# Attention products in two passes, returned pieces split a block earlier, and the sums of the weights sent by another queue

## The chip, the cores and the metric

The kernel runs on one core of a Trainium2 chip. The metric is device time in microseconds (us) for one execution, measured on the slowest core; here there is only one. Engines are called as in the profile: PE is the matrix engine (PEld its weight loads), DVE the vector engine, ACT the scalar engine, POOL the general-purpose engine, SP the engine that in this kernel issues the DMAs. Each has its own instruction queue and works it off in order.

## The reference

Two layers over a sequence of 1024 positions of width 1024, in float32. Layer 0 is a gated linear recurrence. Layer 1, where the change lies, is attention with 16 heads of 64 and a forget gate, and its own output gate:

```python
def fox_mixer(h, w_in, b_f, w_out):
    u = h @ w_in                                    # q, k, v, gate, forget logits
    cum = jnp.cumsum(jax.nn.log_sigmoid(f_logit), axis=1)
    # for each block of 128 queries:
    logits = jnp.einsum("bhqd,bhkd->bhqk", q_blk, kf) * scale
    logits = logits + (cq_blk[..., :, None] - ck[:, :, None, :])
    p = jax.nn.softmax(jnp.where(mask, logits, NEG_INF), axis=-1)
    o = jnp.einsum("bhqk,bkhd->bqhd", p, vf)
    ...
    return (o * jax.nn.silu(gate)) @ w_out
```

Both layers add their result to the residual, and a root-mean-square norm ends the program.

## The kernel before

Precision is kept by splitting: every operand of a large product is cut into a high part and a low part (`to_hi` on ACT, `to_lo` on DVE or POOL), and high times high, low times high and high times low are summed. For the product of attention weights with values, the high and low parts of one weight piece, `ph` and `pl`, are multiplied one after the other with the same stationary tile `v`, which holds high and low values side by side.

Layer 1 goes head by head (`hd` 0 to 15), each head in two halves of 512 queries (`c` = 0 and 1), each half in four rows of 128 queries. Two generators do the work of a half:

- `maxima(hd, c)` computes one row per step: logits `S` on PE, the masked row maximum on DVE (L775), the exponential with its row sum on ACT (L780). For the two longest rows of most halves, `turn_row` then transposes 32x32 blocks on DVE (L735), writes them to DRAM (`turnd`) and reads them back rearranged (`pp<-turnd`): these are the *returned* pieces, called far in the code. After the second half it inverts the eight row sums of the head, turns them on PE (`tr`, L793), copies them to `rc` (L795) and writes them to DRAM (`recd<-rc`, L796).
- `weigh(hd, c)` multiplies weights with values. Pieces of the two shorter rows (and the last piece of the others) are transposed on PE (`pt`), the other pieces come back by DMA. One step of it cuts one or two tiles of pieces into `ph` (ACT, L87) and `pl` (DVE, L98), and issues the products of the step before. `products` goes through the pieces of one step and issues, for each piece, its high product and then its low product into the accumulator `O`.

Between these runs `fill`: the projections of the next heads (`gps`), in steps of six 512-wide products. The order on PE is written out by hand: in a string, `0` is the next step of `weigh`, `1` the next row of `maxima`, `.` a step of fill and of a side task. `ORDER` holds two strings for heads 0 to 11: the first runs `weigh(hd, 0)` beside `maxima(hd, 1)`, the second `weigh(hd, 1)` beside `maxima(hd + 1, 0)`. `LAST` holds those of heads 12 to 15. `tc.issue_after` keeps the PE order as written; the order on ACT, DVE, POOL and SP is otherwise chosen when the program is built, by a planner that places an instruction when it expects its operands to be ready.

The sums come back later: `fetch_sums` (L805) reads `recd` into 64 partitions of `recb`, and `scale` (L815) multiplies the gate `sg` by it, on POOL, in two instructions; `gated` (L915), also on POOL, multiplies the head pair's result `yo` by `sg` after every second head. Both sums' transfers are issued by SP, which also issues every other transfer of the kernel. `settle` calls `fetch_sums` at its third step, behind a transfer of turned rows (`issue_after(written[0].ins)`), and `put_away` calls `scale` in the next head's first run.

Of the kernel before, what the change touches and what calls it, by code (L numbers as in the profile page):

```python
# [23 lines left out]
HD = 64  # L24
EPS = 1e-6
GROUP = 2
ORDER = "1.0..1.10.1.0", "10..1.0.10.10.0"
LAST = "1..0.1..10..1..0", "10..1.0..10..1.0..0"
NEG = -1e30
PSUM = bass.MemoryType.PSUM  # L30
# [8 lines left out]
def trunk(ctx: ExitStack, tc: tile.TileContext, xt, w0, wg, wo0, pc, gn, gf, w1, wv, wf, bf, wo1, out):  # L39
    nc = tc.nc  # L40
# [15 lines left out]
    def matmul(*args, **kw):  # L56
        pe[0] = nc.tensor.matmul(*args, **kw)  # L57
        return pe[0]
# [441 lines left out]
    recd = dram.tile([HEADS, 8, P], F32, name="recd")  # L500

    with ExitStack() as l1:
# [249 lines left out]
        def maxima(hd, c):  # L752

            s = hd % 2
            pair = hd // 2
            if c == 0:
                stats[hd] = at.tile([P, 16], F32, tag="sums", name="sums")[:, :8]
            sums = stats[hd]
            for i in reversed(range(4 * c, 4 * c + 4)):
                n = (i + 1) * P  # L760

                o_ = 192 if i == 4 else 0
                S = ps.tile([P, SEQ], F32, tag="S", name="S")[:, o_:]
                u = U[s][c]
                qs = slice(i % 4 * P, i % 4 * P + P)
                for lo_, hi_ in ((0, min(n, HALF - o_)), (HALF - o_, n)):
                    if hi_ <= lo_:
                        continue
                    hi_ = max(hi_, lo_ + 256)
                    matmul(S[:, lo_:hi_], u[:, 0, qs], T[s][:, 0, lo_:hi_], start=True, stop=False)  # L770
                    matmul(
                        S[:, lo_:hi_], u[:96, 1, qs], T[s][:96, 1, lo_:hi_], start=False, stop=True
                    )
                m = at.tile([P, 1], F32, tag="m", name="m", bufs=4)
                masked[0] = nc.vector.tensor_tensor_reduce(  # L775
                    S[:, :n], S[:, :n], mask[:, SEQ - n :], -1.0, -NEG, ALU.add, ALU.min, accum_out=m
                )

                p = ps_[i] = row_tile(i, n)
                seen[0] = nc.scalar.activation(  # L780
                    p, S[:, :n], AF.Exp, bias=m, scale=-1.0, accum_out=sums[:, i : i + 1]
                )
                if i % 4 > 1 and by_dma(hd, c):
                    turn_row(i, p)
                yield
            if hd == HEADS - 1 or c == 1:
                b0, b1 = (4 * c if hd == HEADS - 1 else 0), 4 * c + 4
                nb = b1 - b0
                sums = sums[:, b0:b1]
                nc.vector.tensor_scalar(sums, sums, 2.0, None, ALU.mult)  # L790
                nc.vector.reciprocal(sums, sums)
                tr = ps.tile([P, P], F32, tag="O", name="tr")
                nc.tensor.transpose(tr[:nb], sums, ident)  # L793
                rc = at.tile([8, P], F32, tag="rc", name="rc", bufs=1)
                nc.vector.tensor_copy(rc[:nb], tr[:nb])  # L795
                nc.sync.dma_start(recd[hd, b0:b1], rc[:nb])  # L796
                if hd > 13:
                    fetch_sums(hd, b0, b1)
                yield

        def fetch_sums(hd, b0=0, b1=8):
            pair, s = hd // 2, hd % 2
            if s == 0:
                recs[pair] = at.tile([P, SEQ], F32, tag="recb", name="recb", bufs=1)
            nc.sync.dma_start(  # L805
                recs[pair][s * HD : (s + 1) * HD, b0 * P : b1 * P],
                recd[hd : hd + 1, b0:b1].rearrange("o b q -> o (b q)").to_broadcast([HD, (b1 - b0) * P]),
            )
# [8 lines left out]
        def weigh(hd, c, sub=slice(0, HALF)):  # L817

            pair, s = hd // 2, hd % 2
            V = Vs[pair]  # L820
            if s == 0:
                yos[pair, c] = at.tile([P, HALF], F32, tag="yo", name="yo", bufs=2)
            yo = yos[pair, c][:, sub]
            O = ps.tile([P, HALF], F32, tag="O", name="O")[:, : sub.stop - sub.start]
            b = 4 * c

            def cover(r0, r1):
                first = [max(j, r0) for j in range(r1)]
                return [(j, (q - b) * P, (r1 - q) * P) for j, q in enumerate(first)]

            def packed(pieces):
                units = []
                for piece in pieces:
                    if not units or sum(w for _, _, w in units[-1]) + piece[2] > HALF:
                        units.append([])
                    units[-1].append(piece)
                return units

            if by_dma(hd, c):
                away = cover(b + 2, b + 4)  # L840
                mine = packed(cover(b, b + 2) + away[-1:])
                away = packed(away[:-1])
            else:
                mine, away = packed(cover(b + sub.start // P, b + sub.stop // P)), []
            steps = [(z[i : i + 2], z is away) for z in (mine, away) for i in range(0, len(z), 2)]
            count = [0, 2 * sum(map(len, mine + away))]

            later = []

            def products(units, parts, far):  # L850
                todo = []
                for unit, (ph, pl) in zip(units, parts):
                    at_ = 0
                    for j, q, w in unit:
                        cs = slice(at_, at_ + w)
                        (later if away and not far and j == b + 3 else todo).append((j, q, w, ph[:, cs], pl[:, cs]))
                        at_ += w
                if far:
                    todo[1:1] = later
                    later.clear()  # L860
                for j, q, w, *z in todo:
                    v = V[j][:, 2 * s : 2 * s + 2].rearrange("p a d -> p (a d)")
                    o = O[:, q - sub.start : q - sub.start + w]
                    for part in z:
                        matmul(o, v, part, start=count[0] == 0, stop=count[0] == count[1] - 1)
                        count[0] += 1

            held = None
            for units, far in steps:
                parts = [[at.tile([P, HALF], F32R, tag=t, name=t, bufs=3) for t in ("ph", "pl")] for _ in units]  # L870
                if not far:
                    A = ps.tile([P, 2, HALF], F32, tag="S", name="pt")
                srcs = []
                for u, unit in enumerate(units):
                    n = sum(w for _, _, w in unit)
                    parts[u] = [z[:, :n] for z in parts[u]]
                    if far:
                        k0, k1 = unit[0][0], unit[-1][0] + 1
                        srcs.append(far_rows(c)[:, :, k0:k1])
                        continue  # L880
                    srcs.append(A[:, u, :n])
                    i = 0
                    for j, q, w in unit:
                        for r in range(b + q // P, b + (q + w) // P):
                            transpose(A[:, u, i : i + P], ps_[r][:, j * P : (j + 1) * P], ident)
                            i += P

                def shaped(z):
                    return z.rearrange("p (k b q) -> p b k q", b=8, q=32) if far else z

                with tc.issue_after((seen if far else pe)[0].ins):
                    for (ph, pl), src in zip(parts, srcs):
                        to_hi(shaped(ph), src, nc.scalar)
                with tc.issue_after((masked if far else pe)[0].ins):
                    for (ph, pl), src in zip(parts, srcs):
                        to_lo(shaped(pl), src, shaped(ph), nc.vector)
                if held:
                    with tc.issue_after(pe[0].ins):
                        products(*held)
                held = units, parts, far  # L900
                yield
            products(*held)

            r0, r1 = s * HD, (1 - s) * HD
            nc.scalar.copy(yo[r0 : r0 + HD], O[r1 : r1 + HD])
            nc.vector.tensor_tensor(yo[r0 : r0 + HD], yo[r0 : r0 + HD], O[r0 : r0 + HD], ALU.add)
            yield
# [219 lines left out]
        for hd in range(HEADS):  # L1127
            pair = hd // 2
            if hd % 2 == 0:
                if hd < 12:  # L1130
                    fill = kq_units(pair + 1, ((1, (0, 1)), (0, (0,))))
                elif hd == 12:
                    pairs = ((0, 1), (2, 3), (4, 5), (6, 7))
                    todo = [(db, c) for two in pairs for c in range(2) for db in two]
# [127 lines left out]
```

## Time and profile before

| what | value |
|---|---|
| time, median of 3 runs | 1110.45 us (1110.2 to 1111.71) |
| the profiled execution, its own time | 1113.33 us |
| its span, first to last instruction | 1111.6 us |
| mean granted PE clock | 0.997 |
| busy: PE, DVE, ACT, POOL | 98%, 71%, 52%, 16% |
| the attention of heads 0 to 11 | about 512 to 941 us of the span |

The profile is one execution. A line of the timeline shows the start in us from the span's start, the length, engine, source line, operation, what it writes and reads, the shape, how many instructions are merged, and in brackets the idle time of the engine just before and what ended it. PE products are pipelined, so their lengths overlap: the distance from one start to the next is what a product costs.

### The profile page before, as it was taken

How to read it: one execution, taken by the hardware profiler on the slowest of the kernel's cores; microseconds unless marked ns; L12 is line 12 of the kernel's file. 1: busy time of each engine (PE TensorE's matmuls, PEld its weight loads, DVE VectorE, ACT ScalarE, POOL GpSimd, SP SyncE). 2: the span in 40 equal slices, each digit the busy share in tenths (PEclk: the TensorE clock that was granted, in tenths of full speed). 3: DMA queues.
4: the chain of work that ended last, by engine and by line, in shares of the span. 5: the costliest groups of instructions: out<-in, count | busy, mean ns of one | idle time of the engine just before them, and what ended most of it. 6: DMA issues, size and time to landing. Idle time of an engine off the chain costs nothing.

```text
span 1111.6 us, 15903 instructions
## 1 busy us (share of the span) xinstructions
PE 1088.2 (98%) x5645; PEld 921.9 (83%) x5645; DVE 785.4 (71%) x1280; ACT 581.3 (52%) x1037; POOL 175.2 (16%) x120
## 2 busy tenths in 40 slices
PE   9999999999999999999999999999999999999997
PEld 7787888888888888988888888888888889888876
DVE  7888755876568687757788477875678765666645
ACT  8487345355453665545555355553555544444435
POOL 2322212111212201420010200202002020110110
PEclk9999999999999999999999999999999999999999
DMA  6111111111112113446767347675376763885445
GB/s 220 62 52 43 51 54 48 43 54 45 49 45 75 48 55 127 130 113 165 199 204 195 116 139 195 198 198 146 107 204 195 202 170 100 251 294 182 138 148 189
DMA packets 100919, 145.81 MB, mean 131 GB/s; under 512 B 25348, under 2 KB 53636, under 8 KB 100840
## 3 DMA queue, kind: packets, MB, share of 16 engines
q1 hardware_dynamic: 100840, 144.80, 44.2%
q8 instruction: 44, 0.72, 0.3%
q14 instruction: 35, 0.29, 0.1%
HBM read 83.48 MB, written 36.11 MB: 108 GB/s over the span
## 4 chain that ended last, share of the span: by engine, by line
PE 75%; DMA 8%; DVE 7%; issue 5%; ACT 3%; SPq 1%; POOL 1%; ACTq 0%; DVEq 0%; POOLq 0%
PE gps L57 24%; PE ops L57 16%; PE ups L57 10%; PE vps L57 8%; PE O L57 5%; PE S L57 4%; PE gate L57 3%; PE turn L57 2%; DMA pp<-turnd 2%; PE pt L61 2%; DMA wf<-in_w 2%; DVE pl L98 2%; DMA turnd<-turn 1%; DVE turn L735 1%; DVE S L775 1%
## 5 line engine op out<-in xcount | busy, mean ns | idle before, releaser
L57 PE MATMUL gps<-hh,wh 128*128 128x512 f32 x576 | 229.8, 399 | 0.3 <-ACT wh L87 0.3
L57 PE MATMUL gps<-hh,wl 128*128 128x512 f32 x576 | 226.2, 393 | 0.0
L57 PE MATMUL gps<-hl,wh 128*128 128x512 f32 x576 | 225.3, 391 | 0.0
L87 ACT CAST wh<-wf 128x512 fp32r<-128x512 f32 (+2 forms) x156 | 94.5, 610 | 152.6 <-PE gps L57 47.8
L98 POOL TENSOR_TENSOR wl<-wf,wh 128x512 fp32r<-128x512 f32 (+1 forms) x60 | 101.9, 1705 | 376.0 <-ACT wh L87 261.4
L57 PEld LDWEIGHTS gps<-hl,wh 128*128 128x128 f32 x576 | 108.5, 188 | 23.5
L57 PEld LDWEIGHTS gps<-hh,wl 128*128 128x128 f32 x576 | 108.8, 189 | 19.6 <-POOL wl L98 0.2
L57 PEld LDWEIGHTS gps<-hh,wh 128*128 128x128 f32 x576 | 108.7, 189 | 19.4 <-ACT wh L87 0.6
L815 POOL TENSOR_TENSOR sg<-sg,recb 64x512 f32<-64x512 f32 x32 | 44.1, 1397 | 494.9 <-DMA recb<-recd 494.9
L775 DVE CUSTOM_DVE_ANT_0 S<-S,mask 128x512 f32<-128x512 f32 (+7 forms) x128 | 97.1, 758 | 25.4 <-PE S L57 24.9
L780 ACT ACTIVATE pp<-S,m 128x512 f32<-128x512 f32 (+1 forms) x64 | 54.4, 850 | 76.8 <-DVE m L775 76.3
L57 PE MATMUL S<-T,U 128*128 128x512 f32 (+7 forms) x384 | 91.4, 346 | 0.0
L57 PE MATMUL O<-pl,v 128*128 128x256 f32 (+3 forms) x302 | 80.3, 301 | 10.8 <-DVE pl L98 10.5
L98 DVE TENSOR_TENSOR wl<-wf,wh 128x512 fp32r<-128x512 f32 x96 | 64.9, 677 | 30.7 <-ACT wh L87 30.5
L375 DVE TENSOR_TENSOR x<-x,ops 128x512 f32<-128x512 f32 x80 | 54.1, 680 | 40.7 <-PE ops L57 40.7
L57 PE MATMUL O<-ph,v 128*128 128x256 f32 (+3 forms) x302 | 80.1, 289 | 1.3 <-ACT ph L87 1.3
L57 PEld LDWEIGHTS S<-T,U 128*128 128x128 f32 (+1 forms) x384 | 68.2, 189 | 12.6 <-ACT pp L780 0.6
L57 PE MATMUL ups<-hh,wl 128*128 128x512 f32 x192 | 75.3, 392 | 0.8 <-POOL wl L98 0.8
L57 PE MATMUL ups<-hh,wh 128*128 128x512 f32 x192 | 75.5, 394 | 0.4 <-ACT hh L89 0.4
L57 PE MATMUL ops<-yh,wh 128*128 128x512 f32 x192 | 75.2, 392 | 0.0
L57 PE MATMUL ups<-hl,wh 128*128 128x512 f32 x192 | 75.1, 391 | 0.1
L57 PE MATMUL ops<-yh,wl 128*128 128x512 f32 x192 | 74.7, 389 | 0.0
(170 smaller groups left out, 2361.8 us busy)
## 6 DMA issues: line engine op xcount, KB each, us to landing
wf<-in_w SPq DMA_DIRECT2D x100, 256.0 KB
turnd<-turn SPq DMA_DIRECT2D x26, 448.0 KB
pp<-turnd SPq DMA_DIRECT2D x52, 224.0 KB
wf<-in_wo SPq DMA_DIRECT2D x64, 128.0 KB
U<-qkh SPq DMA_DIRECT2D x64, 128.0 KB
T<-qkh SPq DMA_DIRECT2D x28, 256.0 KB
turnd<-turn SPq DMA_DIRECT2D x13, 384.0 KB
pp<-turnd SPq DMA_DIRECT2D x52, 96.0 KB
```

The lines of the kernel that those rows point to most:

```text
L57: pe[0] = nc.tensor.matmul(*args, **kw)
L61: pe[0] = nc.tensor.transpose(*args)
L87: nc.scalar.copy(hi, src)
L98: return eng.tensor_tensor(lo, src, f32(hi), ALU.subtract)
L375: nc.vector.tensor_tensor(x, x, pt, ALU.add)
L735: nc.vector.transpose(t[:, 0 if c else r].rearrange("p (m k q) -> p k m q", m=4, q=32), p[:, :n].rearrange("p (k m q) -> p k m q", m=4, q=32),
L775: masked[0] = nc.vector.tensor_tensor_reduce(S[:, :n], S[:, :n], mask[:, SEQ - n :], -1.0, -NEG, ALU.add, ALU.min, accum_out=m)
L780: seen[0] = nc.scalar.activation(p, S[:, :n], AF.Exp, bias=m, scale=-1.0, accum_out=sums[:, i : i + 1])
L815: nc.gpsimd.tensor_tensor(sg, sg, recs[hd // 2][rows, part], ALU.mult)
```

## The change

Three edits. In `products`, a step now issues the high products of all its pieces first and then the low products of all of them, instead of high and low of each piece in turn. In the first string of `ORDER`, the second step of `weigh(hd, 0)`, which cuts the returned pieces and issues the products of the pieces that PE transposed, stands after the second row of `maxima(hd, 1)` instead of after the third; the step of fill that stood between the second and the third row stands behind it. And both transfers of the sums (`recd<-rc` and `recb<-recd`) are issued by POOL's queue instead of SP's, for all 16 heads. An edge that `issue_after` sets binds instructions of the same engine, so the fetch is no longer placed behind the transfer of turned rows on SP.

```diff
-ORDER = "1.0..1.10.1.0", "10..1.0.10.10.0"
+ORDER = "1.0..10.1.1.0", "10..1.0.10.10.0"
...
                 rc = at.tile([8, P], F32, tag="rc", name="rc", bufs=1)
                 nc.vector.tensor_copy(rc[:nb], tr[:nb])
-                nc.sync.dma_start(recd[hd, b0:b1], rc[:nb])
+                nc.gpsimd.dma_start(recd[hd, b0:b1], rc[:nb])
...
-            nc.sync.dma_start(
+            nc.gpsimd.dma_start(
                 recs[pair][s * HD : (s + 1) * HD, b0 * P : b1 * P],
                 recd[hd : hd + 1, b0:b1].rearrange("o b q -> o (b q)").to_broadcast([HD, (b1 - b0) * P]),
             )
...
-                for j, q, w, *z in todo:
-                    v = V[j][:, 2 * s : 2 * s + 2].rearrange("p a d -> p (a d)")
-                    o = O[:, q - sub.start : q - sub.start + w]
-                    for part in z:
-                        matmul(o, v, part, start=count[0] == 0, stop=count[0] == count[1] - 1)
+                for part in range(2):
+                    for j, q, w, *z in todo:
+                        v = V[j][:, 2 * s : 2 * s + 2].rearrange("p a d -> p (a d)")
+                        o = O[:, q - sub.start : q - sub.start + w]
+                        matmul(o, v, z[part], start=count[0] == 0, stop=count[0] == count[1] - 1)
                         count[0] += 1
```

## The prediction

> **What bounds the kernel now.** I read the page first. PE is busy nearly all the time, so time can only be won where PE stands still, and lost where it is made to.
>
> ```profile
> PE 1088.2 (98%) x5645; PEld 921.9 (83%) x5645; DVE 785.4 (71%) x1280; ACT 581.3 (52%) x1037; POOL 175.2 (16%) x120
> ```
>
> The table of waits names the place. Of PE's weight loads, the largest wait by far is that of the products with `pl` for DVE's split:
>
> ```profile
> PEld O L57 <- DVE pl L98: 18.2, 30, 1.0
> ```
>
> So at most some 18 us, 1.6% of the span, are to be had from edits to these products. The timeline of PE shows the dearest form, in the first half (`c` = 0) of a head, the step with the returned pieces:
>
> ```profile
> 544.08 0.28 PE L57 MATMUL O<-ph,v 128*128 128x256 f32 x1
> 545.00 0.39 PE L57 MATMUL O<-pl,v 128*128 128x256 f32 x1 [0.64 <-DVE pl L98]
> 545.22 0.22 PE L57 MATMUL O<-ph,v 128*128 128x128 f32 x1
> 545.28 0.28 PE L57 MATMUL O<-pl,v 128*128 128x128 f32 x1
> 545.40 0.33 PE L57 MATMUL O<-ph,v 128*128 128x256 f32 x1
> ...
> 546.39 0.27 PE L61 MATMUL pt<-ident,p 128*128 128x128 f32 x1
> ```
>
> An undisturbed 256-wide product costs 0.12 us from its start to the next (the 128-wide ones here 0.06 and 0.12). The first low product starts 0.92 after its high one, and the next 0.22 after that: 0.9 lost. It recurs in eight of the eleven first halves of heads 1 to 11; in the other three it is about 0.3:
>
> ```profile
> 602.71 0.28 PE L57 MATMUL O<-ph,v 128*128 128x256 f32 x1
> 603.03 0.39 PE L57 MATMUL O<-pl,v 128*128 128x256 f32 x1
> ```
>
> DVE in the first of the two stretches:
>
> ```profile
> 539.73 0.70 DVE L608 TENSOR_TENSOR gps<-gps,rs 128x512 f32<-128x512 f32 x1 [0.22 <-PE gps L57]
> ...
> 541.32 1.11 DVE L735 STREAM_TRANSPOSE turn<-pp 128x896 f32<-128x896 f32 x1
> 542.35 0.65 DVE L98 TENSOR_TENSOR wl<-wf,wh 128x512 fp32r<-128x512 f32 x1
> 542.92 0.68 DVE L614 SCALAR_TENSOR_TENSOR qkl<-gps,qkh 128x512 fp32r<-128x512 f32 x1
> 543.52 0.82 DVE L775 CUSTOM_DVE_ANT_0 S<-S,mask 128x640 f32<-128x640 f32 x1
> 544.26 0.14 DVE L775 DVE_READ_ACCUMULATOR2_ANT m<- 128x1 f32 x1
> 544.26 1.02 DVE L98 TENSOR_TENSOR pl<-pp,ph 128x512 fp32r<-128x512 f32 x2
> ```
>
> DVE does not rest between 539.73 and 545.28: in this stretch DVE sets the pace, not the place of one instruction in it. The exponential that follows the row maximum of 543.52 is the next thing PE needs (its transposes `pt` at 546.39 read that row):
>
> ```profile
> 544.43 0.79 ACT L780 ACTIVATE p<-S,m 128x640 f32<-128x640 f32 x1 [1.08 <-DVE m L775]
> ```
>
> **The change, part by part.**
>
> *High parts first.* Count and width of the products stay. The weights of a high and a low product are the same `v`, and the new order separates them; the worst that this could cost is the difference between 545.22 to 545.28 (0.06) and 545.28 to 545.40 (0.12), 0.06 for each 128-wide piece, at most four in a head, about 3 us over 12 heads. I take 0: the 0.06 is followed by a dearer start, so that two narrow products together cost their two loads in either order. The gain in a second half, step of ten products:
>
> ```profile
> 556.98 0.29 PE L57 MATMUL O<-ph,v 128*128 128x256 f32 x1
> 557.47 0.39 PE L57 MATMUL O<-pl,v 128*128 128x256 f32 x1 [0.21 <-DVE pl L98]
> ...
> 558.74 0.40 PE L57 MATMUL gps<-hh,wh 128*128 128x512 f32 x1
> ```
>
> ```profile
> 557.54 0.69 DVE L98 TENSOR_TENSOR pl<-pp,ph 128x512 fp32r<-128x512 f32 x1
> 558.72 1.03 DVE L98 TENSOR_TENSOR pl<-pp,ph 128x512 fp32r<-128x512 f32 x2 [0.49 <-ACT ph L87]
> ```
>
> The first wait (0.49 instead of 0.12) goes: five high products, 0.6, now run before the first low one. But the second tile's split ends at 558.23, and after it two low products and a restart (0.24 + 0.14) remain: end 558.62 instead of 558.74. So 0.12 is won, in 12 heads 1.4 us. Bounds: 0, and the whole wait, 0.5 in 12 heads, 6 us.
>
> *Returned pieces split a block sooner.* By high parts alone, a first half would win about 0.35 (four high products, 0.47, instead of one of 0.12 ahead of the first low one). The moved step adds no work but changes DVE's sequence: products of the transposed pieces and one fill step come before the third row, so the fill's result that DVE scales (L608, waiting for PE already) and the third row's `S` come about 0.47 later (four products), while the splits stand ready earlier. If DVE does the splits ahead of the fourth row's maximum, the same list ends with that maximum, at 545.28 + 0.47 = 545.75, and the exponential about 0.95 later, at 546.7; PE, relieved of the 0.9, would come to `pt` at 546.39 - 0.9 = 545.5 and wait 1.2 there: 0.3 worse than now. Or DVE also defers `wl` and `qkl` (0.65 + 0.68) behind the maximum: then nothing is late and the 0.9 is won. Which of them is the planner's choice, which no row shows. Eleven first halves give -8.2 us (8 x 0.9 + 3 x 0.3) to +7 us (0.65 each, if both go before the maximum and the splits too). I take 0: the list of work is the same, DVE has no rest to give, and the wait moves from the low product to `pt`. ACT's two casts only change places with an exponential (ACT has 1.08 of idle time before the next, in the row above), and the returned pieces were sent for in the run before.
>
> *Sums by POOL's queue.* Removed from SP: 34 issues and the waits ahead of them.
>
> ```profile
> SPq L796 <- DVE rc L795: 13.9, 7, 3.0
> ```
>
> Behind these waits stand loads for the next head, which PE does not wait for, and a few weight loads; bounds 0 and 2 us won, I take 0.5, near the first, since PE's largest wait is not on a load. On POOL, behind the two issues stand only `scale` and `gated`. What changes is when `scale` starts. Now, in head 1:
>
> ```profile
> 549.20 0.28 DVE L795 COPY rc<-tr 8x128 f32<-8x128 f32 x1
> ```
>
> ```profile
> 559.48 2.68 POOL L815 TENSOR_TENSOR sg<-sg,recb 64x512 f32<-64x512 f32 x2 [24.61 <-DMA recb<-recd]
> ```
>
> 10.0 after `rc`, and just after the last `pl` split of the second half (558.72 + 1.03). Where the two meet, it is dear:
>
> ```profile
> 618.95 3.42 POOL L815 TENSOR_TENSOR sg<-sg,recb 64x512 f32<-64x512 f32 x2 [26.89 <-DMA recb<-recd]
> ```
>
> ```profile
> 619.66 1.57 DVE L98 TENSOR_TENSOR pl<-pp,ph 128x512 fp32r<-128x512 f32 x1
> ```
>
> 1.57 instead of 0.69: +0.88 for a split beside POOL. The Trainium skill, "SBUF — State Buffer", section "Who interferes with whom", has it that a DVE instruction with two SBUF inputs and a POOL instruction that reads SBUF exclude each other for the whole instruction, whoever comes first; the pair of rows agrees.
>
> How soon will it start? Where SP is not made to wait, late in the run:
>
> ```profile
> 1042.68 0.33 SPq L796 DMA_DIRECT2D recd<-rc  x1
> ...
> 1044.83 0.47 SPq L805 DMA_DIRECT2D recb<-recd  x1
> ```
>
> ```profile
> 1047.86 1.29 POOL L815 TENSOR_TENSOR sg<-sg,recb 64x512 f32<-64x512 f32 x1 [14.45 <-DMA recb<-recd]
> ```
>
> 2.15 to the fetch, 3.03 more to the landing: 5.2. Amid the traffic of head 0, with `rc` done at 522.25:
>
> ```profile
> 521.98 0.27 DVE L795 COPY rc<-tr 8x128 f32<-8x128 f32 x1
> ```
>
> ```profile
> 525.89 1.26 SPq L805 DMA_DIRECT2D recb<-recd  x1
> ```
>
> ```profile
> 532.33 2.54 POOL L815 TENSOR_TENSOR sg<-sg,recb 64x512 f32<-64x512 f32 x2 [45.41 <-DMA recb<-recd]
> ```
>
> ```profile
> 529.70 1.03 DVE L98 TENSOR_TENSOR pl<-pp,ph 128x512 fp32r<-128x512 f32 x2 [0.49 <-ACT ph L87]
> ```
>
> ```profile
> 531.12 0.28 PE L57 MATMUL O<-ph,v 128*128 128x256 f32 x1
> ```
>
> the landing took 6.4. An issue from POOL is not in this trace; I bound it by SP's own issues of `recb<-recd`, 0.47 to 1.26, so 0 to 0.8 more each. The fetch no longer waits behind SP's transfers (in head 0 it was issued 3.6 after `rc`, against 2.15 in the late row), so `scale` starts between 5.2 (the late row) and 10.2 after `rc` (2.15 + 6.4 + 1.6); I take 7.3, nearer to the late row, since the transfers of the sums leave SP's crowded queue, and it lasts 2.7 us. (The skill's "DMA: Bandwidth & Descriptors", section "Latency and other measured facts", gives about 1 us to the first byte for POOL's DMAs against about 0.6 for SP's; by an estimate from that, 0.8 for both, the start would be at 6.0 or later. No run here shows it yet.)
>
> At 7.3 in an even head `scale` meets the two splits of 529.70 (7.5 after `rc`); they end up to 1.7 later, at 532.4 instead of 530.73, and PE, at those products from 531.12 with three high products (0.36) and two low ones (0.24) ahead of the one that needs the second split, stands still for 0.7 at worst; I take 0.5 in six heads: 3 us. In heads 1, 5 and 9 it meets the split of 557.54 (8.1 after `rc`), whose end holds up the last low products of that step: +0.9 in three heads, 2.7 us. In heads 3, 7 and 11, whose splits come later and meet POOL already (619.66), nothing on balance. Sum 5.7 us; bounds 0 (start beyond 9.9) and 15 us (start at 5.5, both splits of the ten-product step hit, about 1.3 in 11 heads).
>
> Sum: -1.4 + 0 + 5.7 - 0.5 (SP) = +3.8 us, on the profiled execution 1113.33 + 3.8 = 1117.1; that execution is 2.9 above the median of 1110.45, so the median becomes 1114.3.
>
> **The rivals.**
>
> *The sums come no sooner than now* (the other side). Place: start of `scale`. If POOL's issues and the landing take together more than 9.9 us in odd heads and 8.6 in even ones, no split is hit, and the products' order has its gain. In first halves this is 0.35 x 8 + 0.3 x 3 = 3.7, with 1.4 and 0.5: 1110.45 - 5.6 = 1104.9; down to 1100 if DVE also defers `wl` and `qkl`. For it: the 6.4 of head 0. Against it: the 5.2 of the late row.
>
> *DVE's sequence decides.* `wl`, `qkl` and the splits all go before the fourth row's maximum, and `pt` waits 0.65 longer than PE lost before, in 11 heads: +7 on top of -1.9 and 5.7, 1121. For it: no DVE rest from 539.73 to 545.28. Against it: 1.07 between the end of the exponential and `pt` now.
>
> *It cancels:* the high parts win about what POOL's earlier start costs: 1110.
>
> **How the numbers follow.** My forecast 0.45 (1111 to 1119), sums late 0.33, DVE's sequence 0.10, cancelling 0.12. Below 1103 and above 1121 I leave 0.1 each: range 1103 to 1121; the likeliest case's own is 1111 to 1119. A change within 0.2% (2.2 us) can hardly be told from none. Slower: 0.38 of the first, 0.10, 0.02; faster: 0.31 of the second, 0.02; the same: the rest, 0.17.
>
> **What would show it.** Right: waits of `O` for `pl` shorter in first halves, but PE idle at `pt` for ACT; `scale` starting 6 to 9 after `rc`; more `pl<-pp,ph` splits of 1.4 us and above than now. Wrong: `scale` still at 9 or later; no wait at `pt`, with `wl` behind the row maximum; or a PE wait for POOL's sums at the end, where the last head's result hangs on them.

## The result and the profile after

| | before | after |
|---|---|---|
| time, median (six runs each) | 1112.5 us | 1121.57 us (1117.7 to 1126.68) |
| ratio, 95% interval | 1 | 1.0085 [1.0065, 1.0106] |
| span of the profiled execution | 1111.6 us | 1119.4 us |

The change costs 9 us. The forecast added 3.8 us to a before of 1110.45, which gives 1114.3, with a range to 1121; here the before measured 1112.5 and 9.1 were added. So the sign was right and the size was not.

The page of the changed kernel shows that PE does the same work, in a longer span:

```profile
PE 1086.8 (97%) x5645; PEld 918.9 (82%) x5645; DVE 787.1 (70%) x1280; ACT 581.4 (52%) x1037; POOL 190.9 (17%) x154
```

Its table of waits (us in total, times, longest):

```profile
PEld pt L61 <- ACT p L780: 18.3, 12, 2.2
PEld O L57 <- DVE pl L98: 11.5, 23, 1.1
...
PE pt L61 <- ACT p L780: 13.1, 12, 1.8
PE O L57 <- DVE pl L98: 6.8, 14, 0.9
```

The wait for `pl`, 18.2 us of weight loads in 30 places before, fell to 11.5 in 23. In its place stands one that the table of before does not hold: the transposes `pt` wait for ACT's exponential, once in each of heads 0 to 11, 13.1 us on PE. The timeline of head 1 shows where it comes from. PE:

```profile
544.67 0.62 PE L57 MATMUL O<-ph,v 128*128 128x256 f32 x4
545.13 0.63 PE L57 MATMUL O<-pl,v 128*128 128x256 f32 x4
545.59 0.63 PE L57 MATMUL S<-T,U 128*128 128x512 f32 x2
547.33 0.33 PE L61 MATMUL pt<-ident,p 128*128 128x128 f32 x1 [1.11 <-ACT p L780]
```

The high and low products now run without a pause: the 0.9 us of before is gone. But `pt` starts at 547.33 (546.39 before). The exponential it needs, on ACT:

```profile
546.39 0.79 ACT L780 ACTIVATE p<-S,m 128x640 f32<-128x640 f32 x1
```

It follows a row maximum on DVE, and DVE has this order:

```profile
540.78 0.70 DVE L608 TENSOR_TENSOR gps<-gps,rs 128x512 f32<-128x512 f32 x1 [0.69 <-PE gps L57]
541.39 1.10 DVE L735 STREAM_TRANSPOSE turn<-pp 128x896 f32<-128x896 f32 x1
542.42 0.94 DVE L775 CUSTOM_DVE_ANT_0 S<-S,mask 128x768 f32<-128x768 f32 x1
...
543.27 1.02 DVE L98 TENSOR_TENSOR pl<-pp,ph 128x512 fp32r<-128x512 f32 x2
544.21 0.69 DVE L98 TENSOR_TENSOR wl<-wf,wh 128x512 fp32r<-128x512 f32 x1
544.81 0.68 DVE L614 SCALAR_TENSOR_TENSOR qkl<-gps,qkh 128x512 fp32r<-128x512 f32 x1
545.41 0.82 DVE L775 CUSTOM_DVE_ANT_0 S<-S,mask 128x640 f32<-128x640 f32 x1
```

Both splits, `wl` and `qkl` stand ahead of the fourth row's maximum (128x640). PE had its `S` done by 543.43, two microseconds before that maximum starts:

```profile
542.67 0.76 PE L57 MATMUL S<-T,U 128*128 128x320 f32 x4
```

DVE also rested 0.69 at `gps` (0.22 before), because the four moved products, 0.47 us, run ahead of that fill step.

Set side by side, the starts of the same PE instructions before and after give the account of each head. At the products of its first half, ahead of the `S` that starts at 545.59 in head 1, PE gains 0.92 us in eight heads and 0.33 in heads 3, 7 and 11, together 8.3. At the `pt` behind that `S` it loses 1.20 to 1.28 in ten heads, 1.93 in head 9 and 0.78 in head 0, together 15.1. Net it loses 6.8.

Another wait is new, on ACT. The copy of a head's result into `yo` waits for an older store of `yo` to land, in heads 2, 4, 6, 8 and 10, and PE then waits a little for the copies that free its accumulator:

```profile
ACT yo L905 <- DMA y1d<-yo: 14.2, 5, 3.2
PE O L57 <- DVE yo L906: 1.2, 4, 0.6
```

POOL in head 1, with the end of the sums' copy on DVE ahead of it:

```profile
552.36 0.28 DVE L795 COPY rc<-tr 8x128 f32<-8x128 f32 x1
```

```profile
552.93 0.57 POOL L796 DMA_DIRECT2D recd<-rc  x1 [16.60 <-DVE rc L795]
556.91 0.54 POOL L805 DMA_DIRECT2D recb<-recd  x1 [3.42 <-DMA recd<-rc]
560.35 2.78 POOL L815 TENSOR_TENSOR sg<-sg,recb 64x512 f32<-64x512 f32 x2 [2.90 <-DMA recb<-recd]
```

```profile
559.70 1.03 DVE L98 TENSOR_TENSOR pl<-pp,ph 128x512 fp32r<-128x512 f32 x2 [0.49 <-ACT ph L87]
...
561.86 1.82 DVE L98 TENSOR_TENSOR wl<-wf,wh 128x512 fp32r<-128x512 f32 x1
```

In this head `scale` starts 7.7 us after `rc` is done (10.0 before); over heads 0 to 11 it starts after 7.5 to 9.5, in the middle 8.6 (9.0 to 11.3, in the middle 9.8, before). In head 1 it stretches no split that PE waits for, but a split of weights, `wl`, of 1.82 instead of 0.69.

### The profile page after: what moved, and what is told of

Its sections match the earlier page's. It is cut to its first block, busy times and chain, and to the rows that moved or that the text cites. A ratio compares the mean times of both kernels' runs of the same rounds, so it can differ in the third digit from the quotient of the medians.

```text
span 1119.4 us, 15903 instructions
## 1 busy us (share of the span) xinstructions
PE 1086.8 (97%) x5645; PEld 918.9 (82%) x5645; DVE 787.1 (70%) x1280; ACT 581.4 (52%) x1037; POOL 190.9 (17%) x154
## 4 chain that ended last, share of the span: by engine, by line
PE 77%; DVE 8%; issue 5%; DMA 4%; ACT 4%; POOL 1%; SPq 1%; DVEq 0%; ACTq 0%; POOLq 0%
PE gps L57 28%; PE ops L57 15%; PE ups L57 10%; PE vps L57 8%; PE S L57 4%; PE O L57 4%; PE gate L57 2%; PE turn L57 2%; PE pt L61 2%; DMA wf<-in_w 2%; DVE pl L98 2%; DVE S L775 2%; ACT p L780 1%; ACT ph L87 1%; DVE wl L98 1%
## 5 line engine op out<-in xcount | busy, mean ns | idle before, releaser
L98 POOL TENSOR_TENSOR wl<-wf,wh 128x512 fp32r<-128x512 f32 (+1 forms) x60 | 99.4, 1661 | 378.8 <-ACT wh L87 262.9
L57 PE MATMUL ops<-yl,wh 128*128 128x512 f32 x192 | 73.6, 389 | 0.0
L57 PE MATMUL vps<-wh,hh 128*128 128x256 f32 (+1 forms) x256 | 72.9, 286 | 0.2 <-DVE x L484 0.2
L57 PE MATMUL vps<-wh,hl 128*128 128x256 f32 (+1 forms) x256 | 72.8, 285 | 0.0
```

The costliest lines, as they stand in the source:

```text
L98: return eng.tensor_tensor(lo, src, f32(hi), ALU.subtract)
```

## The experiments

All runs were timed in five rounds against the kernel before, on the same chip in each group. Ratios below are to that kernel, with their 95% intervals; its median was 1112.67, 1112.51, 1112.78, 1113.81 and 1113.63 us in the five groups.

**Theory A:** the moved split costs, because PE then waits at `pt` for the fourth row's maximum. **Theory B:** the sums by POOL cost, because `scale` meets DVE's splits sooner.

### One part at a time

High parts first alone:

```diff
-                    for part in z:
-                        matmul(o, v, part, ...)
+                for part in range(2):
+                    for j, q, w, *z in todo:
+                        ...
+                        matmul(o, v, z[part], ...)
```

> High products first, nothing else changed. Theory A (the moved block costs, by a wait at the next transposes of PE): this part is a pure gain: in first halves the first low product waits about 0.35 us less in eight heads and not at all in three, in second halves the step of ten products ends 0.1 to 0.2 us sooner; together 4 to 6 us faster than the kernel before, and PE has no wait at the transposes pt. Theory B (the sums by POOL's queue cost): the same 4 to 6 us faster. Rival C (parting high and low products of one weight tile costs weight loads): slower, or no gain, with products of 128 columns 0.05 us dearer each.

1114.17 us, 1.0005 [0.9992, 1.0017]: no gain, where both theories had 4 to 6 us. Yet the starts on PE show it gained as computed, 0.30 to 0.36 in nearly every first half and 0.10 to 0.15 in the steps of ten products. So separating high from low costs nothing that shows, and rival C, which has the time right, has not the reason. PE loses the gain again in a few places, most of it in the second half of head 6. First ACT there, in the kernel before and then with high parts first:

```profile
724.92 0.62 ACT L87 CAST wh<-wf 128x512 fp32r<-128x512 f32 x1 [1.81 <-DMA wf<-in_w]
```

```profile
724.34 0.62 ACT L87 CAST wh<-wf 128x512 fp32r<-128x512 f32 x1 [2.94 <-DMA wf<-in_w]
```

PE was 1.77 ahead by then, but the cast of the weights, which wait for their transfer, came only 0.58 sooner; ACT stood idle 1.13 longer, and behind it on ACT stood an exponential that PE needed:

```profile
725.58 0.50 PE L57 MATMUL S<-T,U 128*128 128x256 f32 x2 [0.98 <-ACT pp L780]
```

Six us later `scale`, which had started after the splits in the kernel before, meets them. Before, DVE and POOL:

```profile
731.04 1.03 DVE L98 TENSOR_TENSOR pl<-pp,ph 128x512 fp32r<-128x512 f32 x2 [0.49 <-ACT ph L87]
```

```profile
732.29 2.53 POOL L815 TENSOR_TENSOR sg<-sg,recb 64x512 f32<-64x512 f32 x2 [23.92 <-DMA recb<-recd]
```

With high parts first:

```profile
730.35 3.21 DVE L98 TENSOR_TENSOR pl<-pp,ph 128x512 fp32r<-128x512 f32 x2 [0.49 <-ACT ph L87]
```

```profile
730.32 2.96 POOL L815 TENSOR_TENSOR sg<-sg,recb 64x512 f32<-64x512 f32 x2 [22.54 <-DMA recb<-recd]
```

Two splits take 3.21 instead of 1.03, and PE waits:

```profile
733.62 0.39 PE L57 MATMUL O<-pl,v 128*128 128x256 f32 x1 [0.90 <-DVE pl L98]
```

The six products of this step take 2.20 us instead of 0.71, so PE loses 1.5 there.

The split one block sooner alone:

```diff
-ORDER = "1.0..1.10.1.0", ...
+ORDER = "1.0..10.1.1.0", ...
```

> Only the moved block (returned pieces split one block sooner), products and queues as before. Theory A: the wait of the low product in first halves goes (0.9 us in eight heads, 0.3 in three), and in its place PE waits 1.0 to 1.2 us at the transposes pt for the exponential of the fourth row, in 11 to 12 heads; with what the earlier products of the transposed pieces may wait, 3 to 8 us slower than before. Theory B: the block is worth its 0.9 us a head or nothing: 0 to 8 us faster, and no wait at pt.

1124.37 us, 1.0099 [1.0078, 1.0121]: 11 us slower, more than the 3 to 8 of theory A. The largest wait of PE is the new one:

```profile
PE pt L61 <- ACT p L780: 12.4, 12, 1.1
```

The sums by POOL alone:

```diff
-                nc.sync.dma_start(recd[hd, b0:b1], rc[:nb])
+                nc.gpsimd.dma_start(recd[hd, b0:b1], rc[:nb])
...
-            nc.sync.dma_start(
+            nc.gpsimd.dma_start(
```

> Only the sums by POOL's queue. Theory A: scale starts 7 to 9 us after rc instead of 9 to 11; a few splits meet it, others no longer do; within 3 us of before, either way. Theory B: 5 to 10 us slower, with more DVE splits pl<-pp,ph of 1.4 us and above than before (seven), or waits of ACT for yo's buffers behind stores to y1d (14 us in the changed kernel).

1116.88 us, 1.0030 [1.0014, 1.0046]: 3.3 us slower, just beyond theory A's 3 and short of theory B's 5 to 10. Eleven splits `pl<-pp,ph` take 1.4 us or more (seven before), as theory B has it. But `scale` starts hardly sooner, in the middle 9.6 us after `rc` for 9.8 before. The waits of ACT for stores to `y1d` are not in this trace.

High parts first and the sooner split, sums by SP (the first two edits):

> The changed kernel with the sums back on SP's queue. Theory A: nearly the changed kernel's time, 5 to 9 us slower than before, and twelve waits of about 1.1 us at pt. Theory B: about the time of e1 or better, 4 to 10 us faster than before.

1123.61 us, 1.0093 [1.0075, 1.0111], with the same wait:

```profile
PE pt L61 <- ACT p L780: 13.3, 12, 1.7
```

That is more than the 5 to 9 us of theory A. So the loss is there with the sums on SP. The queue of POOL on top of it (the changed kernel, 1.0085) adds nothing that these runs can tell.

### Does the place of the fourth row decide?

The same kernel as the last, with the fill step between the third and the fourth row put behind the fourth:

```diff
-ORDER = "1.0..10.1.1.0", ...
+ORDER = "1.0..10.11..0", ...
```

> High parts first and the split moved one block sooner (sums by SP, as before), but the first string is 1.0..10.11..0: the fill step that stood between the third and the fourth row stands behind the fourth row, so that DVE has the fourth row's maximum ahead of wl and qkl. Theory A (PE waits at pt because DVE does wl, qkl and both splits before the fourth row's maximum): the 13 us of waits of pt for ACT's p fall below 4 us, and the time falls from 1123.6 by 8 to 13 us, to 1110 to 1116. Rival (the moved step itself costs, by the rows and fills behind it that come 0.47 later): pt waits go down but the time stays above 1119.

1106.95 us, 0.9951 [0.9933, 0.9969]. No PE wait of `pt` for `p` is left in the table (of the weight loads' waits for it, 2.3 us are). The time falls by 16.7 us. DVE's order in head 1 shows why the wait is gone:

```profile
541.60 0.69 DVE L98 TENSOR_TENSOR pl<-pp,ph 128x512 fp32r<-128x512 f32 x1
542.20 0.83 DVE L775 CUSTOM_DVE_ANT_0 S<-S,mask 128x640 f32<-128x640 f32 x1
...
542.94 0.42 DVE L98 TENSOR_TENSOR pl<-pp,ph 128x256 fp32r<-128x256 f32 x1
543.28 0.68 DVE L98 TENSOR_TENSOR wl<-wf,wh 128x512 fp32r<-128x512 f32 x1
543.88 0.68 DVE L614 SCALAR_TENSOR_TENSOR qkl<-gps,qkh 128x512 fp32r<-128x512 f32 x1
```

The maximum stands behind one split only, and `wl`, `qkl` and the other split follow it. On PE the products, the next `S` and `pt` run back to back:

```profile
543.56 0.63 PE L57 MATMUL O<-pl,v 128*128 128x256 f32 x4
544.02 0.63 PE L57 MATMUL S<-T,U 128*128 128x512 f32 x2
544.49 1.04 PE L61 MATMUL pt<-ident,p 128*128 128x128 f32 x8
```

This kernel is faster than the one before and the changed one; the expected 1110 to 1116 was too high. Theory A holds for the wait: it came from the place of the fourth row in DVE's order and went with it, while the sooner split stayed. The fall of 16.7 is not all this wait. Without `scale`, in the table below, the same edit gains 8.5 us (1.0001 to 0.9925); the rest is a lower price of `scale`.

The fourth row early, and the split behind it (string 1.0..1.110..0):

> High parts first, sums by SP, string 1.0..1.110..0: the fourth row directly behind the third, and the step with the returned pieces behind both. If it is the fourth row's early maximum that brings the gain, and the sooner split too, this is between high parts first alone (1114.2) and 1106.95: 1109 to 1113. If the place of the row alone does it: 1107 or less. If the sooner split does it: 1113 or more.

1120.65 us, 1.0068 [1.0053, 1.0082], slower even than high parts first alone. Of the three cases only the last leaves room for it, and not for its reason. The casts of the returned pieces are bound behind the last exponential that was issued (`issue_after(seen[0].ins)`), which is now the fourth row's:

```profile
544.68 0.80 ACT L780 ACTIVATE p<-S,m 128x640 f32<-128x640 f32 x1 [1.30 <-DVE m L775]
...
545.47 0.91 ACT L87 CAST ph<-pp 128x512 fp32r<-128x512 f32 x2
```

```profile
546.15 0.27 PE L793 MATMUL tr<-ident,sums 128*8 128x128 f32 x1 [0.53 <-ACT ph L87]
```

PE comes for `ph` and waits about 0.5 in eleven heads, 5.8 us together. In this kernel, where the casts hang on the last exponential, row and split have to move together.

The row early and the split sooner, but high and low products in turn:

> String 1.0..10.11..0 and nothing else: products high and low in turn as in the kernel before, sums by SP. High parts first was worth 2.7 us without scale. If it is still so: 1109 to 1112. If the sooner split has taken the stall that high parts first was to cover: 1107 to 1108.5.

1111.32 us, 0.9992 [0.9977, 1.0007]. The interval lies above that of 0.9951, so high parts first is worth about 4.5 us in this order, and the string alone about nothing. The first of the two expected cases.

### What does scale cost?

Seven kernels were run with the multiplications of the gate by the sums left out (transfers stay):

```diff
-                nc.gpsimd.tensor_tensor(sg, sg, recs[hd // 2][rows, part], ALU.mult)
```

The kernel before:

> The kernel before without the multiplications of the gate by the sums on POOL (left out, so the output lacks them); the sums' transfers stay. It is the base for the next two. If POOL's scale stretches splits that PE waits for, it is 1 to 4 us faster than before (the long pl<-pp,ph splits are in heads 3, 7 and 11); otherwise the same.

High parts first alone:

> High parts first alone, also without the multiplications by the sums. Theory (the gain of the high parts, 0.35 in each first half, is given back where scale meets the splits): 3.5 to 5 us faster than the kernel before without them. Rival (given back to loads of weights that arrive at their own time): at most 2 us faster.

The changed kernel:

> The changed kernel, also without the multiplications by the sums. Theory A (the wait at pt is the cost, net of the 0.9 won in first halves about 6 us over 12 heads, less 1.4 for high parts in second halves): 4 to 8 us slower than the kernel before without them. Rival (POOL's scale, started sooner, makes the loss): within 2 us of it.

The sums by POOL alone:

> Sums by POOL's queue alone, without the multiplications of the gate by the sums (left out). Theory (POOL's queue costs only where scale, started sooner, meets the splits): the same as the kernel before without them (1107.67), within 1.5 us. Rival (the transfers by POOL cost by themselves, through the order on SP or where they land): 2.5 us or more above it.

High parts first with the fourth row early:

> High parts first, string 1.0..10.11..0, sums by SP, without the multiplications by the sums (left out). If scale costs as much here as in the kernel before (4.8 us) or the changed one (9): 1098 to 1102. If the long splits, 4.2 us in this kernel's trace in place of 6.7 before, are its whole price: 1103 to 1105.

The same, with the sums by POOL:

> The same with the sums by POOL's queue. Theory (POOL's queue costs only through scale): within 1.5 us of the run with the sums by SP. Rival: 2.5 us or more above it, as 1111.15 against 1106.95 with scale.

High parts first and the sooner split, sums by SP:

> High parts first and the split a block sooner, sums by SP, without the multiplications by the sums (left out): the fourth run's kernel (ratio 1.0093) without scale. Theory (the scale's price rose because the new order shifts the splits against scale, whichever queue carries the sums): the same as the changed kernel without scale, ratio 1.000 within 0.002, so that scale costs 9 to 10 us here too. Rival (it rose because POOL's queue brings the sums sooner): scale costs about 5 us here as in the kernel before, ratio 1.004 or more.

And the string with row 4 early and the sums by POOL, with scale:

> The changed kernel (high parts first, split a block sooner, sums by POOL's queue) with only the string changed to 1.0..10.11..0. Theory A: the wait at pt is gone here too and the time is 1105 to 1110, at least 10 us below the changed kernel. Theory B (sums by POOL cost by themselves, as the 3.3 us of that part alone suggest): 3 us or more above the same string with the sums by SP, 1110 or more.

The last column is the difference of the two ratios times 1112.5 us; each ratio is uncertain by 0.001 to 0.002, so a price by 2 to 3 us.

| kernel | ratio with scale | ratio without | price of scale, us |
|---|---|---|---|
| before | 1 | 0.9955 [0.9940, 0.9970] | 5.0 |
| high parts first | 1.0005 | 0.9927 [0.9911, 0.9942] | 8.7 |
| sums by POOL | 1.0030 | 0.9945 [0.9926, 0.9964] | 9.5 |
| high first, sooner split | 1.0093 | 1.0001 [0.9989, 1.0014] | 10.2 |
| the changed kernel | 1.0085 | 1.0001 [0.9991, 1.0012] | 9.3 |
| high first, row 4 early | 0.9951 | 0.9925 [0.9903, 0.9947] | 2.9 |
| the same, sums by POOL | 0.9985 [0.9973, 0.9998] | 0.9926 [0.9907, 0.9945] | 6.6 |

The kernel with row 4 early and POOL's queue, 1111.15 us, is 10.4 below the changed kernel, as theory A has it, though above the 1105 to 1110 that it named; by the ratios it is 3.8 above the same with SP, as theory B has it. The price before, 5.0, is above the 1 to 4 that was expected; the changed kernel without scale, the two on POOL's queue and the one with the sooner split came out as the theories first named there had it, and the one with row 4 early (1105.13 us) next to the lower of its two prices.

Three things follow. Without scale, POOL's queue makes no difference that these runs can tell in any of the three pairs (before 0.9955 and 0.9945, high first with the sooner split 1.0001 twice, row 4 early 0.9925 and 0.9926): where it costs, it costs through scale. Without scale, high parts first gains 3.1 us, between what its two theories expected: about 3.7 us of its gain went to scale (8.7 less 5.0), and the late weights of head 6 keep 0.6 in the traces without scale. And the changed kernel loses 5.1 us with no scale at all (1.0001 - 0.9955); the other 4.3 are scale's higher price, uncertain by some 3 us, which the same order pays with the sums on SP too. So there the order can raise it without the queue.

The traces with and without scale show where it is paid, in one execution of each. In the changed kernel PE falls behind by 8.0 us from the start of the attention on: 4.5 around the last splits of heads 3, 7 and 11, 1.7 in heads 1, 5 and 9, 0.4 in the even heads, and most of the rest behind head 11. In the kernel before it is 5.0 in all: 4.1 in heads 3, 7 and 11, 0.2 in the even heads, 2.0 behind head 11, less 1.6 at a low product of head 10, which waits 2.22 in the trace without scale for 0.64 with it. Most of the price is thus paid in the same three heads by both.

The same multiplication once for a pair of heads on 128 partitions, in the kernel with row 4 early:

```diff
+            if hd < 12 and hd % 2 == 0:
+                return
-            rows = slice((hd % 2) * HD, (hd % 2 + 1) * HD)
+            rows = slice(0, P) if hd < 12 else slice((hd % 2) * HD, (hd % 2 + 1) * HD)
```

> High parts first, string 1.0..10.11..0, sums by SP, and in heads 0 to 11 the gate is multiplied by the sums once for a pair of heads on 128 partitions instead of once a head on 64. Half of POOL's instructions go, in even heads. If what is left of scale's price lies in splits that it stretches in even and odd heads alike, 1 to 2.5 us faster than 1106.95; if in odd heads alone (there the long splits are), no change within 1 us.

1110.74 us, 0.9972 [0.9956, 0.9989]. It overlaps with 0.9951 [0.9933, 0.9969]: no gain from halving scale shows, and whether it loses is not told.

## Why the prediction was wrong

*High parts first.* The terms were right: 0.12 in steps of ten products (measured 0.10 to 0.15 in most), 0.35 in a first half without the moved split (0.30 to 0.36), 0.9 with it (0.92). That separating high from low costs nothing held as well: the eight products of head 1 take 0.92 us, from 544.67 to 545.59. Taken alone, though, the gain did not reach the end: an earlier PE met `wf` and scale.

*Returned pieces split a block sooner.* This is the step that failed, as the term taken at 0 out of -8.2 to +7. Both branches were worked out, and the planner took the first one: DVE does the splits, and `wl` and `qkl` too, ahead of the maximum. The exponential was put at 546.7 (measured 546.39) and PE's wait at 1.2 (1.11), "0.3 worse than now" (measured 1.25 lost for 0.92 won). The wait itself was named among the signs of being right, and yet nothing was put into the sum for it: by its own 0.3, eight heads should have given +2.4. Then in the three heads where only 0.33 stood to be won the wait at `pt` is as long, 0.95 net each, 2.8 more. Head 9 loses 0.7 more than the others, and head 0, which was not counted, 0.78. Together this is near the 6.8 of the trace, where 0 stood. The upper bound of +7 has the size but not the reason: it puts 0.65 on eleven heads for the order that the text itself had priced at 0.3, and 0.33 was measured in most. (The lower bound, 8 x 0.9 + 3 x 0.3, is -8.1.)

In the changed kernel without scale the whole loss is 5.1 us. To the wait at `pt` come the losses of the even heads; the gain in the steps of ten products is to be taken off. In the traces without scale, PE loses 0.2 to 1.0 us behind the `pt` of heads 2, 4, 6, 8 and 10, together 2.6, and these are the heads where ACT waits for the store of `yo`. The traces of all eleven kernels with the sooner split have this wait, five times each and 14 to 17 us in all; none of the other seven has it. The prediction did not see it. What it costs was not tested by itself.

*The reason for 0* was that the list of work is the same and DVE has no rest to give. The list did not grow, but its order decides who waits: when the split was late, PE lost 0.9; when the maximum is late, PE also waits for the exponential behind it. The string with row 4 early shows that the same list can be put in an order where next to nothing of either is lost.

*Sums by POOL.* This term failed too, though its size looks right by luck: 5.7 us stand beside 4.3. The start of scale was right in head 1, 7.7 for 7.3 after `rc`, but over the heads it is 8.6, and 8.5 to 9.5 in the even ones, where the text itself put no cost beyond 8.6. There it comes behind the splits: by the traces with and without scale, 0.4 us is lost in the even heads, where 3 stood. In heads 1, 5 and 9 it is 1.7, where 2.7 stood, and only head 5 of them has a stretched `pl` split. That heads 3, 7 and 11 change little held, 4.5 for 4.1. Long splits of 1.4 us and above, of which more were expected, are five in the trace, for seven before. The products' new order had moved the splits as well. In head 1, scale begins as the last of them runs and does not stretch it (1.03). It did so before too: the text has it "just after" that split, but 559.48 lies ahead of its end, 558.72 + 1.03. The price rose with the sums on SP too, so in this change the queue cost nothing measurable, though in the kernel before it costs 3.3 and with row 4 early about 3.8. The Trainium skill, "SBUF — State Buffer", section "Who interferes with whom", says that such a pair of DVE and POOL instructions takes turns; 3.21 for 1.03 in head 6, with high parts first, agrees. It does not tell which splits will meet scale, and that is what the sum needed. By the estimate from "DMA: Bandwidth & Descriptors", section "Latency and other measured facts", of the Trainium skill, scale was to start at 6.0 or later; 7.5 to 9.5 agrees, but so would 9.0 to 11.3, that of the kernel before.

*The 0.5 for SP* can't be told from nothing (0.9945 against 0.9955).

*The rivals.* "DVE's sequence decides", with a chance of 0.10, is what happened at `pt`. Its 1121 is the time measured, partly by luck: it adds 10.8 to a base of 1110.45, and 9.1 were measured on 1112.5. It deserved far more: DVE without rest and the row's maximum as next in the chain spoke for it, and only the 1.07 between exponential and `pt` against it (1.17 by the rows shown), which the head's own gain of 0.9 and the later row were bound to use up. "The sums come no sooner" fell in the odd heads, where scale starts 7.5 to 9.3 after `rc`, within its 9.9; in four of the six even heads the start lies beyond its 8.6.

## What to carry to other kernels

When a step is moved earlier, write down the busy engine's new order up to the next thing the bounding engine needs, and price every branch: "the same list of work" is no argument for 0. Where two engines exclude each other, a gain upstream shifts one against the other, and it can be paid back there; a run without the excluded work shows at once how much of a result is such a meeting. And if moving one step makes another late, move that one too: here, with the sums on SP, the row behind the split turned a ratio of 1.0093 into 0.9951, about half of it by a lower price of scale.

## What the runs showed of the hardware

A DMA issued by POOL took 0.57 and 0.54 us of POOL's time in head 1, and POOL then waited another 3.42 and 2.90 us for the landings. From the start of the fetch's issue to the start of scale, POOL's fetches took 3.4 to 6.8 us in heads 0 to 11, in the middle 4.4, and SP's before 3.6 to 6.4, in the middle 5.0: by this trace the queue of POOL is not slower. The price of scale, two POOL instructions of together 2.7 us in a head, off PE's path in the table of waits, ranged from 3 to 10 us of the whole time, with nothing changed but the order and the queue around it. The summed excess of the long `pl` splits does not order these prices (6.7 us in the trace of before, 5.5 in that after). Most of it is paid in heads 3, 7 and 11, but why it differs from kernel to kernel stays open.
